# Weight buffers of one size, a separate load for each unit's last weight quarter, and modulation sums on ScalarE and POOL in a two-layer generator backbone

## The chip, the cores and the metric

The kernel runs on one core of one Trainium2 chip. The core has five engines that run side by side, each its own instructions in order: TensorE (PE; its weight loads are listed as PEld), VectorE (DVE), ScalarE (ACT), GpSimd (POOL) and SyncE (SP), which issues most DMAs. The metric is the time of one execution in device microseconds; lower is better. Three executions of the kernel before took 2499.07, 2501.16 and 2501.43 us, so the median is 2501.16 us.

## The reference

The input is a sequence of 512 latent tokens and 256 context tokens, each with 1024 channels. Two layers follow, then a final normalisation. Each layer computes:

```
sh1, sc1, g1, sh2, sc2, g2 = split(silu(c) @ w_ada[l] + b_ada[l], 6)
h = rmsnorm(x) * (1 + sc1) + sh1
y = hybrid_mixer(h, ...)
x = x + g1 * y
h = rmsnorm(x) * (1 + sc2) + sh2
x = x + g2 * ((silu(h @ w_gate) * (h @ w_up)) @ w_down)
```

The mixer has one input projection (w_in), three branches (windowed attention, a gated linear recurrence, a gated MLP over chunks), a projection of each branch (w_branch) merged by sigmoid gates, and an output projection (w_out). In layer 0 the context tokens go through the same steps with their own modulation vector from c_ctx (so there are two "batches" of modulation, b = 0 and 1); in layer 1 only the latent tokens need the FFN. All is float32. The FFN's inner width is 2816, which is 22 tiles of 128.

## The kernel before, in words

**Layout.** Activations lie channel by token: a tile has 128 channels on the partitions and up to 768 tokens along the row. A matmul takes 128 × 128 weights and up to 512 tokens.

**Three matmuls for one.** Each float32 operand is split into a high and a low part in the matmul's own format (float32r). A product is three matmuls: high weights by high activations, high by low, low by high. For weights the raw tile arrives by DMA in `wr`; ScalarE copies it into `wh`, which rounds it (L288); VectorE subtracts to get `wl` (L289). `dense` (L292) does this for one output tile of 128 channels and `kt` input tiles. For 768 tokens each input tile costs three times (512 + 256) columns of TensorE.

**Weight buffers.** `wr`, `wh` and `wl` are rings (L112 to L114) of 12, 8 and 8 KB a partition. A tile of `kt` = 8 takes 4 KB of a ring, one of 4 takes 2 KB, one of 2 takes 1 KB. A tile that comes round to memory of earlier tiles waits until their last readers are done.

**Layer 0's FFN.** The 22 inner tiles are worked in pieces of 4, 2, 4, 4, 4 and 4 (`FF_PIECES`). A piece first makes its tiles of silu(gate) × up, split in high and low (`gu`), then its down projection: eight output columns of 128 channels, `kt` = the piece's size, each followed by residual adds on VectorE (`add_res`, L780), one for the latent tokens and one for the context. The first piece is plain: gate and up tiles by `dense`. The 18 other tiles are worked in pairs by a scheme with seven products in place of eight: `seven` (L412) takes two weight tiles and two halves of the tokens as a 2 × 2 block product. One call of `seven` is called a unit here; a pair has a gate unit and an up unit.

**A unit.** It loads two raw tiles r1 and r2 of 4 KB a partition (L422); each has a weight tile's two quarters (the upper and the lower half of the input channels). POOL makes four sums, s1 to s4, in this order (L426 to L428), s1 from r2 alone, the others from r1, r2 and earlier sums. `high_low` (L341) splits four stationary tiles: g1 from r1, g2 from s2 and s1, g3 from s3 and s4, and g4 from the second half of r2, which is the last quarter (L450). `product` (L400) runs twelve matmuls of 384 columns for each of the seven products, into three PSUM accumulators, with copies by ScalarE (`ptmp`, L435 to L443) and combinations by VectorE between them. The activations' sums and differences for it come from the generator `seven_acts` (L349), which the plain piece's loop steps; its last step splits four T4 quarters over the memory of the first activation halves, and is taken at the start of the second piece (L1353).

**Modulation.** The products silu(c) @ w_ada are not matmuls, except for the first four units of layer 0. A modulation unit has 512 output columns and four steps (`ada_units`, L527); a step loads 256 rows of w_ada (512 KB, `wra`, also from the ring `wr`) and adds each half, scaled by a channel's silu(c), to an accumulator `acc` (L522 on ScalarE for the very first, L524 on VectorE for the others), for `nb` batches. After the fourth step VectorE folds `acc` down (`ada_fold`, a transpose L499 and a reduction L500 for each batch), and after the last unit `ada_spread` finishes on TensorE and VectorE. The steps wait in `ada_queue`, and `fill(n)` takes n of them wherever the program has room. During layer 0's FFN, 32 steps for layer 1 are queued (L1304): 16 with two batches (units 0 to 3), 16 with one (units 4 to 7). A step is taken after every pair of tiles (L492) and after every second column of a down projection (L1369).

**Order.** The program is written in one order; a planner at build time keeps each engine's queue, moving an instruction ahead where by its own estimate its operands come earlier, with the program's order deciding between those that are ready. On the chip the queues are in order. SP's DMA issues are such a queue too.

## Time and profile before

| | |
|---|---|
| runs, median | 2501.16 us (2499.07 to 2501.43) |
| profiled execution, whole | 2495.73 us |
| its span | 2493.9 us |
| mean granted TensorE clock | 0.992 |
| instructions | 34222 |

The profile shows one execution. Its page gives busy times by engine, 40 slices of the span, DMA queues, the chain that ended last and the costliest groups of instructions; the trace behind it answers questions for a stretch of time: a timeline, a list of waits, busy time by window, groups by shape. Matmuls are pipelined, so the durations of single matmuls overlap, and the distance of their starts is the true pace. `L306` is the matmul of `dense`, `L407` that of a unit. In a row such as `pd<-hh,wl` the output stands left of the arrow and the operands right of it. Numbers in square brackets in a timeline are the engine's idle time before the row and what ended it. Slices of 62 us of the page, TensorE, VectorE and DMA:

```profile
PE   8899999999999989989999999999999999999998
DVE  4688777875534376666656586678884547433335
DMA  8222111123523232233233252111213645233334
```

Layer 0's FFN runs from about 920 to 1480 us of the span: slices 15 to 24.

### The profile page before, as it was taken

The numbers are of one execution on the slowest core, as the hardware profiler recorded it, in microseconds if no ns is written. First come the engines' busy times: TensorE is split into PE (matmuls) and PEld (weight loads), VectorE is DVE, ScalarE is ACT, GpSimd is POOL, SyncE is SP. The second block draws the span as 40 slices with busy tenths as digits, with TensorE's granted clock in tenths as the row PEclk, the third lists the DMA queues.
The fourth block names the chain that finished last, engine by engine and source line by source line (L and its number), as shares of the span: only waits on it lengthen the run. The fifth ranks groups of instructions, "written<-read, shape, count | busy, mean of one in ns | idle before, by whom it ended". The sixth has DMA issues, their size and how long they took to land. (4 is left out here: it accounts for less than half of the span.)

```text
span 2493.9 us, 34222 instructions
## 1 busy us (share of the span) xinstructions
PE 2400.1 (96%) x13606; PEld 2084.2 (84%) x13606; DVE 1548.0 (62%) x2636; ACT 896.0 (36%) x1508; POOL 321.4 (13%) x223
## 2 busy tenths in 40 slices
PE   8899999999999989989999999999999999999998
PEld 3888888888888878879998978888888789887888
DVE  4688777875534376666656586678884547433335
ACT  3333354442222343232423453335453325322224
POOL 0000100000111230221212231000000122000001
PEclk9999999999999999999999999999999999999999
DMA  8222111123523232233233252111213645233334
GB/s 289 70 77 77 52 43 40 38 64 106 156 86 88 80 98 85 81 94 113 78 109 110 77 160 60 43 43 52 60 52 118 182 136 155 85 100 94 93 99 129
DMA packets 360080, 235.28 MB, mean 94 GB/s; under 512 B 8369, under 2 KB 331377, under 8 KB 359921
## 3 DMA queue, kind: packets, MB, share of 16 engines
q1 hardware_dynamic: 355984, 220.52, 30.0%
q0 software_dynamic: 2304, 10.49, 1.2%
q8 instruction: 107, 1.75, 0.3%
q10 hardware_dynamic: 1632, 2.10, 0.2%
q14 instruction: 53, 0.43, 0.1%
HBM read 225.73 MB, written 7.34 MB: 93 GB/s over the span
## 5 line engine op out<-in xcount | busy, mean ns | idle before, releaser
L288 ACT ACTIVATE wh<-wr 128x1024 fp32r<-128x1024 f32 (+4 forms) x344 | 306.5, 895 | 804.8 <-PE pd L306 655.9
L289 DVE TENSOR_TENSOR wl<-wr,wh 128x1024 fp32r<-128x1024 f32 (+4 forms) x344 | 353.1, 1030 | 260.4 <-ACT wh L288 257.5
L306 PE MATMUL pd<-hh,wh 128*128 128x512 f32 (+1 forms) x1504 | 458.6, 361 | 0.2 <-DVE q L793 0.2
L306 PE MATMUL pd<-hh,wl 128*128 128x512 f32 (+1 forms) x1504 | 448.3, 354 | 10.5 <-DVE wl L289 10.3
L306 PE MATMUL pd<-hl,wh 128*128 128x512 f32 (+1 forms) x1504 | 447.0, 354 | 0.0
L306 PEld LDWEIGHTS pd<-hh,wl 128*128 128x128 f32 x1504 | 248.3, 190 | 51.7 <-DVE wl L289 13.9
L306 PEld LDWEIGHTS pd<-hl,wh 128*128 128x128 f32 x1504 | 247.9, 190 | 33.8
L306 PEld LDWEIGHTS pd<-hh,wh 128*128 128x128 f32 x1504 | 248.4, 190 | 30.3 <-issue 0.9
L524 DVE SCALAR_TENSOR_TENSOR acc<-wra,sc,acc 128x512 f32<-128x512 f32 x224 | 165.9, 766 | 97.8 <-DMA wra<-in_w_ada 78.6
L306 PE MATMUL pd<-fl,wh 128*128 128x512 f32 (+1 forms) x496 | 176.8, 373 | 4.5 <-DVE fl L703 4.5
L306 PE MATMUL pd<-fh,wh 128*128 128x512 f32 (+1 forms) x496 | 175.7, 372 | 4.0 <-ACT wh L288 3.4
L306 PE MATMUL pd<-guh,wh 128*128 128x512 f32 (+1 forms) x576 | 174.4, 344 | 3.9 <-DVE X L780 1.9
L306 PE MATMUL pd<-fh,wl 128*128 128x512 f32 (+1 forms) x496 | 175.5, 371 | 0.3 <-DVE wl L289 0.3
L306 PE MATMUL pd<-guh,wl 128*128 128x512 f32 (+1 forms) x576 | 173.4, 343 | 2.4 <-DVE wl L289 2.3
L306 PE MATMUL pd<-gul,wh 128*128 128x512 f32 (+1 forms) x576 | 173.6, 342 | 0.0
L780 DVE SCALAR_TENSOR_TENSOR X<-pd,mod,X 128x256 f32<-128x256 f32 (+1 forms) x160 | 84.2, 559 | 98.9 <-PE pd L306 98.4
L306 PEld LDWEIGHTS pd<-guh,wh 128*128 128x128 f32 x576 | 99.3, 190 | 18.0 <-ACT guh L732 2.2
L306 PEld LDWEIGHTS pd<-guh,wl 128*128 128x128 f32 x576 | 99.4, 191 | 15.8 <-DVE wl L289 3.2
L306 PEld LDWEIGHTS pd<-gul,wh 128*128 128x128 f32 x576 | 99.4, 190 | 14.2 <-DVE gul L733 1.4
L306 PEld LDWEIGHTS pd<-fh,wh 128*128 128x128 f32 x496 | 89.9, 189 | 22.8 <-ACT wh L288 6.0
L306 PEld LDWEIGHTS pd<-fl,wh 128*128 128x128 f32 x496 | 90.4, 189 | 21.4 <-DVE fl L703 5.8
L652 POOL TENSOR_TENSOR sqa<-sqa,sq 128x256 f32<-128x256 f32 (+1 forms) x40 | 51.6, 1290 | 417.9 <-ACT sq L650 412.9
(285 smaller groups left out, 4478.0 us busy)
## 6 DMA issues: line engine op xcount, KB each, us to landing
wr<-in_w_in SPq DMA_DIRECT2D x116, 512.0 KB, 3.8
wra<-in_w_ada SPq DMA_DIRECT2D x80, 512.0 KB, 3.8
wr<-in_w_ffn_gate SPq DMA_DIRECT2D x44, 512.0 KB, 3.8
wr<-in_w_ffn_up SPq DMA_DIRECT2D x44, 512.0 KB, 3.9
wr<-in_w_out SPq DMA_DIRECT2D x32, 512.0 KB, 3.7
wr<-in_w_branch SPq DMA_DIRECT2D x48, 256.0 KB, 3.4
wr<-in_w_ffn_down SPq DMA_DIRECT2D x48, 256.0 KB, 3.4
wr<-in_w_ffn_down SPq DMA_DIRECT2D x24, 384.0 KB, 3.2
```

Of the source, the lines that this page charges most:

```text
L288: nc.scalar.activation(out=h, in_=r, func=AF.Copy)
L289: nc.vector.tensor_tensor(out=o, in0=r, in1=h.bitcast(F32), op=ALU.subtract)
L306: nc.tensor.matmul(ps[:, b0:b1], lhsT=w[:, k, :], rhs=x[:, b0:b1], start=b not in first, stop=(k == kt - 1 and i == 2), skip_group_check=True)
L524: nc.vector.scalar_tensor_tensor(out=acc[:, 0:512], in0=w, scalar=sc, in1=acc[:, 0:512], op0=ALU.mult, op1=ALU.add)
L652: eng.tensor_tensor(out=acc[:, c0:c1], in0=acc[:, c0:c1], in1=sq[:, c0:c1], op=ALU.add)
L780: self.nc.vector.scalar_tensor_tensor(out=self.X[m][:, c0:c1], in0=ps[:, c0:c1], scalar=gcol(b, m), in1=self.X[m][:, c0:c1], op0=ALU.mult, ...
```

## The change

- The rings become pools of fixed places: three for `wr`, two for `wh`, two for `wl`, each 4 KB a partition, with one tag, so that a smaller tile occupies a whole place (`load_raw`, `stationary`).
- A unit loads its last weight quarter a second time, as a tile r3 of its own (256 KB), and g4 is split from r3 in place of the second half of r2.
- No modulation step is taken in `seven_gate_up` any more. In layer 0 one is taken after every second column only in pieces of more than two tiles.
- The four one-batch units 4 to 7 go to a queue of their own, `pool_queue`, taken after the other columns of those pieces. Their products are made by ScalarE (into a page `acm`) and added by POOL; the first one goes straight into the accumulator. The fold of such a unit comes one step later, at the start of the next unit, with an extra step at the end. The sums of each group have a `parts` tile of their own size.
- The last step of `seven_acts` is taken at the end of the first piece's gate and up tiles, ahead of its down projection.

```diff
-        self.wr = ctx.enter_context(tc.tile_pool(name="wraw", bufs=1)).ring(3 * D * 4, name="wrawr")
-        self.wh = ctx.enter_context(tc.tile_pool(name="whi", bufs=1)).ring(2 * D * 4, name="whir")
-        self.wl = ctx.enter_context(tc.tile_pool(name="wlo", bufs=1)).ring(2 * D * 4, name="wlor")
+        self.wr = ctx.enter_context(tc.tile_pool(name="wraw", bufs=3))
+        self.wh = ctx.enter_context(tc.tile_pool(name="whi", bufs=2))
+        self.wl = ctx.enter_context(tc.tile_pool(name="wlo", bufs=2))
...
     def load_raw(self, wap, kt):
-        raw = self.wr.tile([P, kt, P], F32, name=self.nm("wr"))
+        raw = self.wr.tile([P, KD, P], F32, tag="wr", name=self.nm("wr"))[:, 0:kt, :]
...
+    def stationary(self, kt):
+        return [pool.tile([P, KD, P], F32R, tag=tag, name=self.nm(tag))[:, 0:kt, :]
+                for pool, tag in ((self.wh, "wh"), (self.wl, "wl"))]
...
         r1, r2 = (self.load_raw(w, KD).rearrange("p k c -> p (k c)") for w in (w1, w2))
+        r3 = self.load_raw(w2[KD // 2 * P:, :], KD // 2).rearrange("p k c -> p (k c)")
...
-        g4 = self.high_low(r2[:, n:2 * n])
+        g4 = self.high_low(r3)
...
             self.free(s)
-            self.fill(1)
...
-            else:
+            elif eng is None:
                 nc.vector.scalar_tensor_tensor(out=acc[:, 0:512], in0=w, scalar=sc, in1=acc[:, 0:512],
                                                op0=ALU.mult, op1=ALU.add)
+            else:
+                t = self.single("acm")
+                nc.scalar.activation(out=t[:, 0:512], in_=w, func=AF.Copy, scale=sc)
+                eng.tensor_tensor(out=acc[:, 0:512], in0=acc[:, 0:512], in1=t[:, 0:512], op=ALU.add)
+                self.free(t)
...
+            j = i if lag == 0 else i - 1
+            if q == (3 if lag == 0 else 0) and j >= 0:
+                for b, acc in enumerate(state[j]):
+                    r0 = 16 * (j * nb + b)
+                    self.ada_fold(acc, state["parts"][:, r0:r0 + 16])
...
-            self.ada_queue += self.ada_units(1, (0, 1, 2, 3), 2) + self.ada_units(1, (4, 5, 6, 7), 1)
+            self.ada_queue += self.ada_units(1, (0, 1, 2, 3), 2)
+            self.pool_queue = self.ada_units(1, (4, 5, 6, 7), 1, nc.gpsimd)
...
-            if l == 0 and f0 + n > plain:
-                if f0 <= plain:
-                    quarters, qheld = next(making)
+            if l == 0 and f0 + n == plain:
+                quarters, qheld = next(making)
+            elif l == 0:
                 self.seven_gate_up(l, range(max(f0, plain), f0 + n, 2), quarters, gu, guheld)
...
-                    if l == 1 or m % 2:
+                    if l == 1 or m % 2 and n > 2:
                         self.fill(1)
+                    elif n > 2 and self.pool_queue:
+                        self.pool_queue.pop(0)()
```

More of the change, by code (lines that the diff above doesn't have):

```diff
@@ L284, in load_w @@
         raw = self.load_raw(wap, kt)
-        hi = self.wh.tile([P, kt, P], F32R, name=self.nm("wh"))
-        lo = self.wl.tile([P, kt, P], F32R, name=self.nm("wl"))
+        hi, lo = self.stationary(kt)
         r, h, o = (t.rearrange("p k c -> p (k c)") for t in (raw, hi, lo))
@@ L529, in ada_units @@
+    def ada_units(self, l, units, nb, eng=None):
         state = {}
+        tag = "parts" if eng is None else "partsp"
+        lag = 0 if eng is None else 1
         def step(i, q):
-            u = units[i]
+            u = units[i] if i < len(units) else None
             if (i, q) == (0, 0):
-                self.parts = self.sp.tile([P, 128], F32, tag="parts", name=self.nm("parts"))
-            if q == 0:
-                state["accs"] = [self.single("acc") for _ in range(nb)]
-            raw = self.wr.tile([P, 2, 512], F32, name=self.nm("wra"))
@@ L538, in step @@
-            self.nc.sync.dma_start(out=raw, in_=self.a["w_ada"][l][q * 256:(q + 1) * 256, u * 512:(u + 1) * 512]
-                                   .rearrange("(k p) c -> p k c", p=P))
-            for k in (0, 1):
-                self.ada_accum(state["accs"], raw[:, k, :], 2 * q + k)
-            if q == 3:
-                for b, acc in enumerate(state["accs"]):
-                    r0 = 16 * (i * nb + b)
-                    self.ada_fold(acc, self.parts[:, r0:r0 + 16])
-                self.free(*state["accs"])
-                if i == len(units) - 1:
-                    self.ada_spread(l, units, self.parts, nb)
@@ L549, in ada_units @@
-        return [lambda i=i, q=q: step(i, q) for i in range(len(units)) for q in range(4)]
+                state["parts"] = self.sp.tile([P, 16 * nb * len(units)], F32, tag=tag, name=self.nm(tag))
+            if u is not None:
+                if q == 0:
+                    state[i] = [self.single("acc") for _ in range(nb)]
+                raw = self.wr.tile([P, 2, 512], F32, tag="wr", name=self.nm("wra"))
+                self.nc.sync.dma_start(out=raw, in_=self.a["w_ada"][l][q * 256:(q + 1) * 256, u * 512:(u + 1) * 512]
+                                       .rearrange("(k p) c -> p k c", p=P))
+                for k in (0, 1):
+                    self.ada_accum(state[i], raw[:, k, :], 2 * q + k, eng)
@@ new lines, in step @@
+            j = i if lag == 0 else i - 1
[3 more added lines that the diff above has]
+                    self.ada_fold(acc, state["parts"][:, r0:r0 + 16])
+                self.free(*state[j])
+                if j == len(units) - 1:
+                    self.ada_spread(l, units, state["parts"], nb)
+        steps = [(i, q) for i in range(len(units)) for q in range(4)] + [(len(units), 0)] * lag
@@ L551, in ada_first @@
+        return [lambda i=i, q=q: step(i, q) for i, q in steps]
     def ada_first(self):
```

6 lines of the change are left out of this document (2 added, 4 removed).

## The prediction

> **What bounds the kernel now.** I read the busy times first, then what TensorE waits for, then the stretches of the layer-0 FFN, the only place where the order of work changes. Busy times, page part 1:
>
> ```profile
> PE 2400.1 (96%) x13606; PEld 2084.2 (84%) x13606; DVE 1548.0 (62%) x2636; ACT 896.0 (36%) x1508; POOL 321.4 (13%) x223
> ```
>
> TensorE is the bound: 2400.1 of 2493.9 us. No edit takes a matmul away, so only its 94 us of idle time, and time at a lower clock, can move. The list of TensorE's waits from 920 to 1490 us (layer 0's FFN; us in total, times, longest), then the same list from 1049 to 1082 us, the FFN's short piece of two tiles:
>
> ```profile
> PE pa L407 <- ACT ptmp L435: 7.9, 5, 2.6
> PE pa L407 <- DVE wl L733: 7.1, 10, 1.6
> ...
> PE pd L306 <- DVE wl L289: 2.3, 1, 2.3
> PE pd L306 <- ACT guh L732: 1.9, 1, 1.9
> PE pd L306 <- DVE X L780: 1.3, 2, 0.8
> ```
>
> L407 is a product of a seven-product unit: 7.9 + 7.1 = 15.0 us are lost in the units, 2.3 + 1.9 + 1.3 = 5.5 us in and before the short piece's down projection. The longest wait, in the timeline (POOL, ACT, PE; start, us, idle before and releaser):
>
> ```profile
> 1113.17 1.87 POOL L428 TENSOR_TENSOR s<-wr 128x512 f32<-128x512 f32 x1 [17.20 <-DMA wr<-in_w_ffn_gate]
> 1118.28 1.06 ACT L732 ACTIVATE wh<-s 128x1024 fp32r<-128x1024 f32 x1 [4.63 <-POOL s L428]
> 1116.68 0.33 PE L407 MATMUL pb<-fh,wh 128*128 128x384 f32 x1
> ...
> 1117.55 0.34 PE L407 MATMUL pb<-fh,wl 128*128 128x384 f32 x1
> 1120.49 0.76 PE L407 MATMUL pa<-np,wh 128*128 128x384 f32 x2 [2.60 <-ACT ptmp L435]
> ```
>
> POOL waits for the second raw weight tile (r2) of the next gate unit, ScalarE for POOL's sums, TensorE for ScalarE (2.60). From 1116.68 to 1117.55 are five matmuls, 0.174 us each; a product of twelve takes 2.1. r2 is late because the tile whose place it takes is held until the up unit before it splits its last quarter. The waits cost clock too; granted clock by windows of 3.4 us (the column after POOL):
>
> ```profile
> 1055.90:1059.30 3.40, 3.40 (x13) 2.60 (x12) 3.10 (x5) 0.80 (x2) 0.00 (x0) 0.51 0.00 0
> 1076.40:1079.80 3.40, 3.40 (x11) 2.92 (x12) 2.15 (x5) 1.06 (x1) 0.00 (x0) 0.50 0.66 191
> 1120.80:1124.20 3.40, 3.40 (x12) 3.40 (x11) 2.35 (x3) 1.12 (x2) 0.60 (x1) 0.50 0.51 151
> 1219.80:1223.20 3.40, 3.40 (x12) 3.40 (x11) 3.40 (x12) 0.90 (x2) 2.41 (x2) 0.50 0.02 6
> ```
>
> Half clock for 3.4 us costs 1.7 us of work; four times 1.7 is 6.8 us. (The Trainium skill, "TensorE: Matmul & The Clock Gate", section "Why this matters for your kernels", asks only for no idle gaps over about 3 us; here gaps of 1.9 to 2.6 us were followed by half clock, so the rows decide, and the rule has no chance of its own. By it the change would win 6.8 us less and come out near 2517.)
>
> **What goes.** The third load r3 frees r2 as soon as POOL has summed it, so the next unit's r1 and r2 land a whole unit earlier; and the one modulation step after each pair of tiles, whose products stand in VectorE's queue ahead of weight splits (0.99 us of waiting for its DMA, then 0.75, before a split), leaves the units:
>
> ```profile
> 1097.37 0.75 DVE L524 SCALAR_TENSOR_TENSOR acc<-wra,sc,acc 128x512 f32<-128x512 f32 x1 [0.99 <-DMA wra<-in_w_ada]
> 1098.04 1.22 DVE L733 TENSOR_TENSOR wl<-wr,wh 128x1024 fp32r<-128x1024 f32 x1
> ```
>
> The short piece gets no steps at all. At most 15.0 + 5.5 + 6.8 = 27.3 us go. I take 25: a little over two of the 15 are waits at a unit's first product behind a down projection, which neither edit touches.
>
> **What comes.** The steps gather in the four down projections of four tiles before the last piece: four two-batch steps (VectorE) and four one-batch steps (ScalarE and POOL) in each, where it had four in all. And every raw tile, a down tile of 2 KB a partition too, now fills one of three 4 KB places, and one of two for wh and wl. Prices:
>
> ```profile
> wra<-in_w_ada SPq DMA_DIRECT2D x80, 512.0 KB, 3.8
> wr<-in_w_ffn_gate SPq DMA_DIRECT2D x44, 512.0 KB, 3.8
> ...
> wr<-in_w_ffn_down SPq DMA_DIRECT2D x48, 256.0 KB, 3.4
> L288 ACT ACTIVATE wh<-wr 128x512 fp32r<-128x512 f32 x96 | 60.0, 630 | 144.1 <-PE pd L306 110.2 <-DMA wr<-in_w_ffn_down 19.8 <-PE pg L407 10.5
> L289 DVE TENSOR_TENSOR wl<-wr,wh 128x512 fp32r<-128x512 f32 x96 | 68.1, 714 | 6.3 <-ACT wh L288 6.3
> L522 ACT ACTIVATE acc<-wra,sc 128x512 f32<-128x512 f32 x32 | 22.1, 718 | 33.6 <-DMA wra<-in_w_ada 31.4 <-DVE macc L1290 0.8 <-PE pd L306 0.7
> L524 DVE SCALAR_TENSOR_TENSOR acc<-wra,sc,acc 128x512 f32<-128x512 f32 x224 | 165.9, 766 | 97.8 <-DMA wra<-in_w_ada 78.6 <-ACT acc L522 18.7
> L499 DVE STREAM_TRANSPOSE tr<-acc 128x512 f32<-128x512 f32 x32 | 21.2, 691 | 0.1
> L500 DVE TENSOR_REDUCE parts<-tr 128x16 f32<-128x512 f32 x32 | 20.6, 666 | 0.2
> L780 DVE SCALAR_TENSOR_TENSOR X<-pd,mod,X 128x256 f32<-128x256 f32 x112 | 51.6, 478 | 57.0 <-PE pd L306 56.8
> L780 DVE SCALAR_TENSOR_TENSOR X<-pd,mod,X 128x512 f32<-128x512 f32 x48 | 35.9, 748 | 41.9 <-PE pd L306 41.6
> L428 POOL TENSOR_TENSOR s<-wr,wr 128x512 f32<-128x512 f32 x18 | 27.5, 1529 | 4.1 <-DMA wr<-in_w_ffn_up 4.1
> ```
>
> And one such down projection now, VectorE's first and last residual add (X) and some rows between; then the engines' busy time in it:
>
> ```profile
> 994.60 1.14 DVE L780 SCALAR_TENSOR_TENSOR X<-pd,mod,X 128x512 f32<-128x512 f32 x2 [1.06 <-PE pd L306]
> 995.66 0.68 DVE L289 TENSOR_TENSOR wl<-wr,wh 128x512 fp32r<-128x512 f32 x1
> 996.85 2.74 DVE L524 SCALAR_TENSOR_TENSOR acc<-wra,sc,acc 128x512 f32<-128x512 f32 x4 [0.51 <-DMA wra<-in_w_ada]
> ...
> 1016.86 2.25 DVE L733 TENSOR_TENSOR wl<-wr,wh 128x1024 fp32r<-128x1024 f32 x1
> ...
> 1024.28 1.14 DVE L780 SCALAR_TENSOR_TENSOR X<-pd,mod,X 128x512 f32<-128x512 f32 x2 [3.10 <-PE pd L306]
> ```
>
> ```profile
> 990.00:1023.50 33.50, 33.50 (x191) 29.00 (x190) 23.68 (x36) 5.55 (x8) 6.08 (x4) 1.00 0.33 97
> ```
>
> Seven columns in 1024.28 − 994.60: 4.24 us each, without a stall. The next unit's r1 is already being split at 1016.86, some seven microseconds ahead of need; that lead is what the small tiles buy.
>
> *Places.* A down tile holds its place 3.4 + 0.63 + 0.71 = 4.7 us, a ScalarE step's tile 3.8 + 2 × 0.72 = 5.2, a VectorE step's 3.8 + 4 × 0.77 and one column's residual adds between (0.75 + 0.48) = 8.1. Two columns need 2 × 4.7 + 5.2 + 8.1 = 22.7 us of places; three places give 3 × 8.48 = 25.4. Booked: 89%. Now it is two 2 KB tiles and one 4 KB tile in 12 KB: (2 × 2 × 4.7 + 4 × 8.1) / 12 = 4.3 of 8.48 us, 51%. VectorE's own load there is 8 × (0.75 + 0.48 + 0.71) + 14 × 0.77 + 3 folds × 1.36 = 30.4 of 33.9 us, 90%. Nothing breaks in the mean; queues form.
>
> *Start of the next unit (four times).* r2 takes the place of the last down tile. That tile's wh and wl wait for column 5 to end (two places; columns count from 0), then 0.63, residual adds 1.23, 0.71: 2.6 us. r2 lands 3.8 later; two POOL sums 3.1, wh 1.06, wl 1.22: 11.8 us after column 5. TensorE wants that wl after two columns, two products and two matmuls, 8.5 + 4.2 + 0.35 = 13.0: 1.2 us to spare, or 1.9 late with one block of four modulation products (3.06) ahead of the tile's split. VectorE is also late by itself. The last step's tile takes the place of down tile 6: column 4's end + 2.6 + 3.8, which is 2.2 us after column 5. In the 10.8 us that are left VectorE has, in program order, the block 3.06, adds 2.46, the last down split 0.71, folds 3 × 1.36 and the unit's first two splits 2.44: 12.8 us, so 2.0 late, and about 3 with a DMA wait like the 0.5 and 1.0 in the rows above. I take 3.5, between this and both latenesses together (4.9), and 1.7 of clock, since shorter gaps brought it: 4 × 5.2 = 20.8 us. Ends: 0 (as now, where the lead covers it) and 4 × (4.9 + 1.7) = 26.
>
> *Inside the down projection.* With two places for wl, a split may start when the column two before ends and is needed 4.2 + 0.7 us later; 0.63 goes to ScalarE. VectorE has 4.2 us for a block 3.06, adds 1.23, split 0.71: 5.0, over by 0.8, and by 1.9 with a DMA wait. Half of the four blocks meet it: 2 × 1.3 = 2.6 a projection, 10.4 us in all. Ends 0 and 16 × 1.9 = 30. The merge stage (595 to 850 us), with two places for wl and one such block for a gate and a branch column today, has
>
> ```profile
> PE pd L306 <- DVE wl L289: 4.9, 3, 2.5
> ```
>
> which is 1.6 us each where it happens, between my 0.8 and 1.9.
>
> *The rest.* 28 products go from VectorE (0.77 each) to ScalarE (0.72) and POOL (about 1.5, from L428): both are idle for four fifths of the row above (5.55 and 6.08 of 33.5); without cover 0.7 us each. POOL's adds slow a neighbour: the split at 1016.86 took 2.25 us beside POOL's sums, against 1.22 above. I count 3 us in all, ends −2 and 11. (The Trainium skill, "SBUF — State Buffer", section "Who interferes with whom", says that a VectorE operation with two SBUF inputs and a POOL operation that reads SBUF block each other; the 2.25 agrees.) The 18 loads r3 add 4.7 MB on SP's queue behind loads that wait for places; the units need three loads per 14.5 us, so nothing. The quarters' splits (T4), moved ahead of the first down projection, wait for the last plain unit's matmuls, as they do now: nothing. Layer 1's down projections lose a raw place but have no steps: nothing, at most 4.
>
> *Sum.* −25 + 20.8 + 10.4 + 3 = +9.2 us: on the profiled execution's 2495.7 (span 2493.9 and 1.8 around it) 2504.9; that execution was 5.4 below the median of the runs, so 2501.2 + 9.2, or 2510.
>
> **Rivals.** *Main (0.40):* as summed; its own range is 2506 to 2522.
> *The places are enough (0.25; the other side):* if modulation tiles are consumed as they land, so that r2 is issued before column 5 has ended, the start of the units costs 1 us each, the down projections 0.5 each, the rest 1: 7 − 25 = −18, 2483. It decides where the fold falls: at 12.8 us of queue in 10.8 it fails, with the folds (4.1) done earlier it holds. For it: the unstalled row of today.
> *Even (0.20):* 3 and half a clock window a start (15.4), 1 a projection (4), the rest 3, so 22.4 − 25: 2499.
> *POOL blocks VectorE (0.10):* seven adds a projection, each adding 1.0 us (2.25 − 1.22), bring VectorE to 30.4 + 7 = 37.4 of 33.9 us: 3.5 more for each, 14 in all: 2524. For it, the 2.25; against, the modulation products' mean of 766 ns.
> *r3 doesn't bring r2 forward (0.05):* POOL's sums need pages that come free no earlier; about 15 of the gain stays away: 2525.
>
> **Numbers.** Slower: 0.40 + 0.10 + 0.05 = 0.55; same: 0.20; faster: 0.25, with the line at 0.2% (5 us), about what a measurement of this kernel can tell from no change. The range runs from inside the faster case to the two slow ones: 2485 to 2527.
>
> **What would show it.** The waits for `ptmp` and `wl` in units that follow units gone; new waits of 2 to 5 us for `wh` or `wl` where a unit follows a down projection, with half clock behind; TensorE waiting for `wl` (L289's line) in those projections; SP waiting longer for modulation products. If these starts are clean, the sum of places is wrong; if the second pairs still wait, r3 is.

## The result, and the profile after

The changed kernel took 2484.41 us (median of four runs, 2477.91 to 2485.28), the kernel before in the same runs 2500.39 (2499.07 to 2501.43). The ratio is 0.9931, with a 95% interval from 0.9913 to 0.9949: **faster by 16 us, 0.7%**, where I had forecast 9 us slower. The profiled execution took 2485.11 us, its span is 2483.3. Busy times, the page's part 1:

```profile
PE 2401.9 (97%) x13606; PEld 2085.3 (84%) x13606; DVE 1533.7 (62%) x2608; ACT 919.2 (37%) x1536; POOL 368.8 (15%) x251
```

The engines do the work that the diff says: 28 modulation products left VectorE. The list of TensorE's waits from 920 to 1480 us, layer 0's FFN (us in total, times, longest):

```profile
PE pg L409 <- ACT wh L744: 7.9, 3, 3.6
PE pd L309 <- DVE wl L292: 5.1, 4, 3.3
...
PE ada L511 <- DVE parts L502: 2.8, 1, 2.8
PE pa L409 <- ACT ptmp L438: 1.2, 1, 1.2
...
PE pa L409 <- DVE wl L745: 0.8, 2, 0.5
```

L409 is the product of a unit (L407 before), L309 the matmul of `dense` (L306). The 7.9 and 7.1 us of waits inside the units are 1.2 and 0.8. New are the first and the third row: the starts of the four units that follow a down projection (in the fourth, matmuls that finish the modulation, `ada`, stand ahead of the unit and wait for the last fold). The second row has nothing to do with them: 4.6 of its 5.1 us are a wait of 1.31 us in the last column of the stage and one of 3.33 at layer 1's first projection, where the kernel before waits 4.38 us for squares of the next norm (sqa) instead. One of the four starts, in the timeline of all engines (start, us, engine; in brackets the idle time before the row and what ended it):

```profile
1155.33 6.77 SPq L279 DMA_DIRECT2D wr<-in_w_ffn_gate  x3
...
1158.97 2.74 DVE L526 SCALAR_TENSOR_TENSOR acc<-wra,sc,acc 128x512 f32<-128x512 f32 x4 [2.36 <-DMA wra<-in_w_ada]
1161.03 1.06 ACT L744 ACTIVATE wh<-wr 128x1024 fp32r<-128x1024 f32 x1 [5.33 <-DMA wr<-in_w_ffn_gate]
...
1162.47 1.29 POOL L431 TENSOR_TENSOR s<-wr 128x512 f32<-128x512 f32 x1 [6.47 <-DMA wr<-in_w_ffn_gate]
1162.67 1.29 DVE L501 STREAM_TRANSPOSE tr<-acc 128x512 f32<-128x512 f32 x2
...
1163.89 1.24 DVE L502 TENSOR_REDUCE parts<-tr 128x16 f32<-128x512 f32 x2
1165.05 1.21 DVE L745 TENSOR_TENSOR wl<-wr,wh 128x1024 fp32r<-128x1024 f32 x1
...
1165.14 1.06 ACT L744 ACTIVATE wh<-s 128x1024 fp32r<-128x1024 f32 x1 [3.06 <-DVE parts L502]
...
1166.25 1.01 PE L409 MATMUL pg<-np,wh 128*128 128x384 f32 x2 [2.24 <-ACT wh L744]
```

Two chains end together. VectorE has the block of four products, the residual adds and two folds ahead of the split of r1: its wl ends at 1165.05 + 1.21 = 1166.26. r2 landed at 1162.47, POOL's two sums took until 1165.1, and the wh made of them ends at 1165.14 + 1.06 = 1166.20. TensorE waits 2.24 us. The granted clock behind three of these starts, by windows (PE, PEld, DVE, ACT, POOL busy, then the clock):

```profile
1166.30:1169.70 3.40, 3.40 (x11) 3.40 (x12) 2.18 (x3) 0.00 (x0) 3.32 (x2) 0.50 0.28 77
1265.30:1268.70 3.40, 3.40 (x13) 3.40 (x12) 1.42 (x2) 0.47 (x1) 2.55 (x2) 0.50 0.49 143
1360.80:1364.20 3.40, 2.96 (x12) 2.96 (x13) 3.40 (x9) 1.06 (x1) 3.17 (x3) 0.51 0.01 2
1364.20:1367.60 3.40, 3.40 (x13) 3.40 (x12) 2.68 (x17) 0.00 (x0) 0.48 (x1) 0.50 0.83 235
```

The last two rows are one start: its half clock lasts 6.8 us, two windows of 3.4.

So the gain in the units came and so did the late starts. To see what else moved, I cut every profiled execution at the same matmuls (each trace lists 13606): the 3601st, 5201st, 8801st, 10801st, 12001st and the 13601st. The stretches are layer 0's merge, layer 0's FFN with the first tiles of layer 1, then layer 1's merge and FFN; in brackets stands the time at half clock, counted in windows of 3.4 us (it comes in pieces of 3.4 or 6.8 us but for the run's very end). The last columns give the median and the ratio to the kernel before, run beside it. Medians are of the fast runs; four slow ones (2533 and 6038 us of wr_ring, 4746 of raw_places_alone, 9584 of dve_units) are left out, with which those three medians would be 2494.86, 2488.86 and 2487.32.

| kernel | merge 0 | FFN 0 | merge 1 | FFN 1 | median us | ratio (95%) |
|---|---|---|---|---|---|---|
| before | 293.3 (1) | 669.8 (6) | 231.9 (1) | 334.3 | 2500.39 | |
| after | 288.5 (0) | 666.6 (8) | 237.1 (1) | 328.6 | 2484.41 | 0.9931 (0.9913 to 0.9949) |
| pools_alone | 288.4 (0) | 663.5 (4) | 238.5 (2) | 328.6 | 2485.72 | 0.9948 (0.9933 to 0.9962) |
| rings_kept | 294.0 (1) | 645.6 (2) | 239.4 (3) | 334.3 | 2482.43 | 0.9932 (0.9918 to 0.9947) |
| no_r3 | 288.4 (0) | 659.7 (7) | 238.0 (2) | 328.6 | 2480.31 | 0.9925 (0.9909 to 0.9941) |
| mod_old | 288.4 (0) | 669.4 (4) | 236.9 (1) | 328.6 | 2485.26 | 0.9944 (0.9929 to 0.9959) |
| mods_alone | 291.4 (0) | 657.5 (4) | 238.5 (2) | 334.3 | 2490.20 | 0.9961 (0.9950 to 0.9973) |
| r3_alone | 296.3 (2) | 668.4 (6) | 232.8 (0) | 334.3 | 2500.17 | 1.0003 (0.9994 to 1.0012) |
| raw_places_alone | 285.1 (0) | 669.5 (7) | 237.1 (1) | 334.4 | 2487.20 | 0.9953 (0.9937 to 0.9969) |
| wr_ring | 292.5 (1) | 663.7 (4) | 241.9 (4) | 328.6 | 2492.99 | 0.9977 (0.9966 to 0.9988) |
| wr_ring_dve | 295.5 (3) | 653.5 (4) | 239.1 (2) | 328.6 | 2485.37 | 0.9952 (0.9940 to 0.9965) |
| wh_wl_rings | 285.1 (0) | 650.8 (4) | 234.0 (0) | 334.3 | 2470.78 | 0.9895 (0.9877 to 0.9912) |
| wh_wl_no_r3 | 285.1 (0) | 649.6 (2) | 236.4 (2) | 334.3 | 2477.36 | 0.9910 (0.9892 to 0.9928) |
| wh_wl_dve | 288.4 (0) | 645.0 (3) | 235.4 (0) | 334.3 | 2468.93 | 0.9881 (0.9868 to 0.9894) |
| whole_l1 | 289.9 (1) | 653.5 (4) | 234.3 (0) | 328.6 | 2469.50 | 0.9881 (0.9864 to 0.9898) |
| lag_all | 288.5 (0) | 658.6 (3) | 240.6 (1) | 328.6 | 2480.34 | 0.9914 (0.9896 to 0.9932) |
| wl_ring | 288.4 (0) | 663.6 (8) | 237.6 (1) | 333.1 | 2487.83 | 0.9942 (0.9921 to 0.9963) |
| dve_units | 285.1 (0) | 666.8 (9) | 239.6 (2) | 328.6 | 2485.16 | 0.9938 (0.9916 to 0.9960) |
| both_gains | 289.9 (1) | 646.5 (4) | 236.0 (1) | 328.6 | 2463.16 | 0.9847 (0.9823 to 0.9872) |

From before to after, in the two profiled executions: merge 0 −4.8 us, FFN 0 −3.2, merge 1 +5.2, FFN 1 −5.7. In the merges and in layer 1's FFN nothing of the change is at work but the buffers, and my sum had no term there.

Each stretch can be taken apart further: TensorE's waits, the work lost at half clock (1.7 us a window), and the rest, which is the pace of the matmuls. FFN 0 is 35.6 + 10.2 + 624.0 us before and 29.6 + 13.7 + 623.3 after. Layer 0's merge is 6.7 + 1.7 + 284.8 before and 1.8 + 0 + 286.6 after, so waits and clock gave 6.6 us there and the pace took 1.8 back. The pace is not the change's: in dve_units, whose instructions of that stretch are the same, in the same order on TensorE, it is 283.2 (a hundred of the first thousand matmuls take 17.33 us there and 17.67 in the changed kernel). What sets it stays open; it moves a single profile by 3.4 us.

### The profile page after: what moved, and what is told of

Same layout as the page of the kernel before. It is cut to its first block, busy times and chain, and to the rows that moved or that the text cites. A ratio compares the mean times of both kernels' runs of the same rounds, so it can differ in the third digit from the quotient of the medians.

```text
span 2483.3 us, 34425 instructions
## 1 busy us (share of the span) xinstructions
PE 2401.9 (97%) x13606; PEld 2085.3 (84%) x13606; DVE 1533.7 (62%) x2608; ACT 919.2 (37%) x1536; POOL 368.8 (15%) x251
## 4 chain that ended last, share of the span: by engine, by line
PE 58%; DVE 10%; DMA 5%; issue 4%; ACT 2%; POOL 1%; POOLq 0%; DVEq 0%; ACTq 0%
PE pd L309 43%; PE pa L409 6%; DMA wra<-in_w_ada 5%; PE pg L409 3%; DVE wl L292 3%; DVE acc L526 2%; PE pb L409 1%; PE hl L857 1%; ACT wh L291 1%; DVE X L792 1%; PE pT L1117 1%; PE sc L1062 1%; DVE fl L715 1%; DVE nt L705 0%; PE pv L1108 0%
## 5 line engine op out<-in xcount | busy, mean ns | idle before, releaser
L309 PE MATMUL pd<-hh,wl 128*128 128x512 f32 (+1 forms) x1504 | 451.9, 356 | 11.0 <-DVE wl L292 11.0
L309 PE MATMUL pd<-hh,wh 128*128 128x512 f32 (+1 forms) x1504 | 459.0, 361 | 0.8 <-ACT wh L291 0.6
L309 PE MATMUL pd<-hl,wh 128*128 128x512 f32 (+1 forms) x1504 | 446.2, 353 | 0.0
L309 PEld LDWEIGHTS pd<-hh,wl 128*128 128x128 f32 x1504 | 248.4, 189 | 53.0 <-DVE wl L292 16.2
L309 PEld LDWEIGHTS pd<-hh,wh 128*128 128x128 f32 x1504 | 249.2, 190 | 33.1 <-ACT wh L291 2.0
L309 PEld LDWEIGHTS pd<-hl,wh 128*128 128x128 f32 x1504 | 247.2, 189 | 34.6
L526 DVE SCALAR_TENSOR_TENSOR acc<-wra,sc,acc 128x512 f32<-128x512 f32 x196 | 142.1, 761 | 158.7 <-DMA wra<-in_w_ada 122.8
L309 PE MATMUL pd<-fl,wh 128*128 128x512 f32 (+1 forms) x496 | 177.2, 373 | 4.6 <-DVE fl L715 4.6
L309 PE MATMUL pd<-fh,wl 128*128 128x512 f32 (+1 forms) x496 | 176.3, 372 | 0.4 <-DVE wl L292 0.3
L309 PE MATMUL pd<-fh,wh 128*128 128x512 f32 (+1 forms) x496 | 175.3, 371 | 0.6 <-ACT silu L1351 0.6
L309 PE MATMUL pd<-guh,wh 128*128 128x512 f32 (+1 forms) x576 | 174.2, 343 | 0.9 <-ACT wh L291 0.5
L309 PE MATMUL pd<-guh,wl 128*128 128x512 f32 (+1 forms) x576 | 172.8, 341 | 1.8 <-DVE wl L292 1.8
L309 PE MATMUL pd<-gul,wh 128*128 128x512 f32 (+1 forms) x576 | 173.2, 341 | 0.3 <-DVE gul L745 0.2
L309 PEld LDWEIGHTS pd<-guh,wl 128*128 128x128 f32 x576 | 98.3, 189 | 15.5 <-DVE wl L292 2.6
L309 PEld LDWEIGHTS pd<-gul,wh 128*128 128x128 f32 x576 | 98.9, 189 | 14.7 <-DVE gul L745 1.6
L309 PEld LDWEIGHTS pd<-guh,wh 128*128 128x128 f32 x576 | 98.5, 189 | 14.4 <-ACT wh L291 1.2
L309 PEld LDWEIGHTS pd<-fl,wh 128*128 128x128 f32 x496 | 90.6, 189 | 21.8 <-DVE fl L715 5.8
L309 PEld LDWEIGHTS pd<-fh,wl 128*128 128x128 f32 x496 | 90.9, 190 | 17.3 <-DVE wl L292 1.2
```

Source lines behind the costliest of these rows:

```text
L309: nc.tensor.matmul(ps[:, b0:b1], lhsT=w[:, k, :], rhs=x[:, b0:b1], start=b not in first, stop=(k == kt - 1 and i == 2), skip_group_check=True)
L526: nc.vector.scalar_tensor_tensor(out=acc[:, 0:512], in0=w, scalar=sc, in1=acc[:, 0:512], op0=ALU.mult, op1=ALU.add)
```

## The experiments

**The parts of the change, each put back or done alone.** First, the kernel before with fixed places for all three buffers (pools_alone), then the changed kernel with rings again (rings_kept), without the third load (no_r3), and with the old modulation steps (mod_old).

```diff
 pools_alone, on the kernel before (rings_kept: the reverse, on the changed one)
-        self.wr = ctx.enter_context(tc.tile_pool(name="wraw", bufs=1)).ring(3 * D * 4, name="wrawr")
+        self.wr = ctx.enter_context(tc.tile_pool(name="wraw", bufs=3))
...
 no_r3, on the changed kernel
-        r3 = self.load_raw(w2[KD // 2 * P:, :], KD // 2).rearrange("p k c -> p (k c)")
-        g4 = self.high_low(r3)
+        g4 = self.high_low(r2[:, n:2 * n])
...
 mod_old, on the changed kernel
+            self.fill(1)
-            self.ada_queue += self.ada_units(1, (0, 1, 2, 3), 2)
-            self.pool_queue = self.ada_units(1, (4, 5, 6, 7), 1, nc.gpsimd)
+            self.ada_queue += self.ada_units(1, (0, 1, 2, 3), 2) + self.ada_units(1, (4, 5, 6, 7), 1)
-                    if l == 1 or m % 2 and n > 2:
+                    if l == 1 or m % 2:
```

> The kernel before with one edit: the three rings become pools of fixed 4 KB places (three, two, two). Theory 'places help outside layer 0's FFN': the waits for wl in layer 0's merge (1.8 + 0.5 + 2.5 us and a half-clock window, together 5.7) and the 3.4 us at the returns from layer 1's down projections to its gate and up tiles go, 5 us come in layer 1's merge, and layer 0's FFN, whose units still wait for r2 and for steps, loses up to 10 from raw places held longer: 2495 to 2505. Rival 'places only cost' (the gains in the merge and in layer 1 come from elsewhere): 2505 to 2515, with the waits in layer 0's merge still there.

> The changed kernel with the rings put back; r3 and the placing of the modulation steps stay. Theory 'places help outside layer 0's FFN, and cost at the starts of its units': the starts behind the four down projections (2.1 to 3.6 us each, 15.8 with the clock) shrink to about half, the merge of layer 0 and layer 1's transitions lose 11 and layer 1's merge wins 5 again: 2480 to 2486. Rival 'places only cost': 2465 to 2475. Rival 'without places r3 helps less, since a tile comes round to memory in the order of the ring': 2490 or more, with waits for wl or ptmp inside the units.

> The changed kernel without the third load: g4 is split from the second half of r2 again. Theory 'r2 held until g4 makes the next unit's r2 late': the units that follow another unit wait for ptmp and wl again, about 10 of the 15 us and some half clock come back: 2494 to 2500. Rival 'the modulation steps in the units made them wait': 2483 to 2487, no waits inside the units.

> The changed kernel with the modulation steps where they were: one after each pair of tiles, one after every second column of every down projection, all products on VectorE; pools, r3 and the earlier T4 splits stay. Theory 'the steps gathered in the down projections make the next unit's start late': the four starts lose their 2.1 to 3.6 us waits and the half clock (up to 15.8 us less), while a step between the units costs what it did, 3 to 8 us: 2474 to 2482. Rival 'the units need VectorE and the places free of steps': 2490 to 2500, with waits for ptmp and wl in the units.

Measured: 2485.72, 2482.43, 2480.31 and 2485.26 us. Each of the four is within 5 us of the whole change, so its parts do not add. Places alone give most of it (13.4 us below the kernel before that ran beside them), with 6.3 us from layer 0's FFN, which no theory of mine had. Rings kept give as much, but from one stretch: FFN 0 falls by 24.2 us. Its waits there, TensorE's list from 920 to 1480 us, hold no start of a unit at all (gul is the low part of silu(gate) × up, X the residual):

```profile
PE pd L309 <- DVE gul L745: 2.9, 4, 0.9
PE pd L309 <- DVE X L792: 1.1, 2, 0.8
```

Against rings, fixed places cost layer 0's FFN 666.6 − 645.6 = 21.0 us, and what they give lies in the other stretches. Without the third load the waits in the units did not come back, against my theory; the starts were late by 7.7 us in sum, not 10.7. With the old steps neither theory's time came: the late starts went, and the units waited 7.6 us for wl in their place.

**The third load and the moved steps, each with rings.** mods_alone is rings_kept without r3; r3_alone is the kernel before with r3 as its one edit.

> The kernel before with the modulation steps placed and made as in the change (none in the units, one-batch ones on ScalarE and POOL) and the earlier T4 splits; rings, and no third load. Theory 'the steps in the units, not the hold on r2, made the units wait' (places without the third load had no such waits either): the 15.0 us of waits for ptmp and wl and the 5.5 of the short piece go, 2478 to 2486. Rival 'r2 held until the last quarter is split makes the next unit late': about 10 of the 15 us and their half clock stay, 2488 to 2494.

> The kernel before with one edit: the third load. Theory 'the steps in the units made them wait': the waits inside the units stay at 10 to 15 us, 2495 to 2502. Rival 'r2 held until the last quarter is split makes the next unit late': they fall below 5 us, 2484 to 2491.

2490.20 and 2500.17 us: the third load alone does nothing. Its list for layer 0's FFN shows the waits of the units as they were (L407 is a unit's product):

```profile
PE pa L407 <- ACT ptmp L436: 8.5, 5, 2.6
PE pa L407 <- DVE wl L734: 6.0, 8, 1.1
```

and that of mods_alone shows them nearly gone, with others in the down projections:

```profile
PE pd L309 <- DVE X L791: 4.8, 5, 1.6
...
PE pd L309 <- DVE gul L744: 4.4, 5, 1.3
PE pa L409 <- DVE wl L744: 2.0, 4, 1.0
PE pa L409 <- ACT ptmp L437: 1.4, 2, 1.0
```

So with the steps between the units they wait, 14.5 us even with r3, and without the steps 3.4. The earlier T4 splits, which mods_alone has too, are not the reason: mod_old keeps them, and with the steps back its units waited for wl again. But the hold on r2 is not disproved. The split of the last quarter and the issue of the next gate unit's r2, first in the kernel before, then in r3_alone (there two loads, r3 at 1110.78 and r2 at 1111.46):

```profile
1107.94 0.69 DVE L733 TENSOR_TENSOR wl<-wr,wh 128x512 fp32r<-128x512 f32 x1 [2.29 <-ACT wh L732]
1108.66 0.37 SPq L279 DMA_DIRECT2D wr<-in_w_ffn_gate  x1
```

```profile
1110.74 0.69 DVE L734 TENSOR_TENSOR wl<-wr,wh 128x512 fp32r<-128x512 f32 x1
1110.78 1.05 SPq L279 DMA_DIRECT2D wr<-in_w_ffn_gate  x2
```

In both, r2 is issued 0.03 us after that split ends. In r3_alone the split reads r3, which lies in the same ring: r2's load now waits for the split of r3 and is as late as before (the wait behind it is 2.60 us in both). A step's tile, also in the ring, is loaded between the two units in both kernels. Without it (mods_alone) most of the wait is gone though r2 is held as before, so the hold cost what it did together with the step.

The time of mods_alone lies in the rival's range all the same, because 9.2 us of waits for X and gul came. With the steps gone, r3 on top gives 657.5 − 645.6 = 11.9 us in FFN 0, 3.4 of it half clock; the waits for X and gul fall to 4.0. How the third load shortens those was not taken apart.

**Which buffer.** wr_ring is the changed kernel with a ring for raw tiles alone, wh_wl_rings with rings for wh and wl alone, raw_places_alone the kernel before with fixed places for raw tiles alone, wl_ring the changed one with a ring for wl alone.

```diff
 wr_ring
-        self.wr = ctx.enter_context(tc.tile_pool(name="wraw", bufs=3))
+        self.wr = ctx.enter_context(tc.tile_pool(name="wraw", bufs=1)).ring(3 * D * 4, name="wrawr")
...
 wh_wl_rings
-        self.wh = ctx.enter_context(tc.tile_pool(name="whi", bufs=2))
-        self.wl = ctx.enter_context(tc.tile_pool(name="wlo", bufs=2))
+        self.wh = ctx.enter_context(tc.tile_pool(name="whi", bufs=1)).ring(2 * D * 4, name="whir")
+        self.wl = ctx.enter_context(tc.tile_pool(name="wlo", bufs=1)).ring(2 * D * 4, name="wlor")
```

> The changed kernel with the raw tiles' buffer (wr) a ring again; wh and wl keep two fixed places. With rings for all three, layer 0's FFN lay 24 us below the kernel before and no unit started late behind a down projection; with places for all it lay only 3 to 4 below; but the places took 4 to 6 us of waits for wl out of layer 0's merge and 5.7 us of waits for wh out of layer 1's FFN. Theory 'raw places cost the lead of the next unit's loads, places for wh and wl pay elsewhere': starts clean, merge and layer 1 as with places: 2470 to 2476, below every kernel so far. Rival 'two places for wh and wl make the starts late': 2481 to 2486, with waits of 2 to 3.5 us at the starts behind the four down projections.

> The changed kernel with rings for wh and wl and fixed places for raw tiles, the mirror of the run before. Theory 'raw places cost the lead': starts behind the four down projections still 2 to 3.5 us late, and the waits for wl in layer 0's merge and for wh (3.4 us in six) in layer 1's FFN are back: 2486 to 2494. Rival 'two places for wh and wl make the starts late': starts clean, 2479 to 2484.

> The kernel before with one edit: fixed places for the raw tiles only; wh and wl stay rings, the modulation steps and the second half of r2 as before. Theory 'in a ring of raw tiles the loads of the modulation steps land later than VectorE's queue has them, and splits stand behind them' (with raw places the two waits of about 1.8 us for wl in layer 0's merge were gone, with a ring they were there in each kernel): the merge of layer 0 is 5 to 8 us shorter, the units' waits in its FFN stay: 2489 to 2495. Rival 'raw places help only where the steps have been moved': 2496 to 2502.

> The changed kernel with a ring for wl alone; raw tiles and wh keep fixed places. Theory 'either of the two holds the last down tile until column 5 has ended': wh's places are enough for it, the starts stay 2 to 3.5 us late: 2482 to 2486. Rival 'only the split into wl counts, since it is the raw tile's last reader': starts clean, 2466 to 2473.

2492.99, 2470.78, 2487.20 and 2487.83 us. My theory for the first pair fell: with the steps moved, places for the raw tiles are the good part, those for wh and wl the bad one in layer 0's FFN (in layer 1's they are worth 5.7 us, below). Behind the four down projections no first product of a unit waits more than 0.4 us in either kernel of the pair, so a late start needs places for raw tiles and for wh and wl together. In wr_ring the product that needs r2's sums still waits, 4.7 us in the four units (for ptmp and wl). This fits the chain of the prediction, where r2 takes the place of the last down tile, which waits for wh and wl, which wait for column 5; either edit opens it. One link is looser than I had it. In the start shown above column 5 ended at about 1154.5, but the last tile's split into wh waited last for the tile's own load, whose place a block of products had held until 1152.27:

```profile
1155.06 0.63 ACT L291 ACTIVATE wh<-wr 128x512 fp32r<-128x512 f32 x1 [1.59 <-DMA wr<-in_w_ffn_down]
```

In layer 0's FFN wh_wl_rings is 666.6 − 650.8 = 15.8 us below the changed kernel: 6.8 of waits, 6.8 of half clock and 2.1 of pace. The late starts' 10.7 us of waits are gone, but its down projections wait 6.7 us for gul and X, which the changed kernel's don't. With a ring for wl alone the wh places hold the last tile as before, and the starts are late again; its list, layer 0's FFN:

```profile
PE pg L409 <- ACT wh L744: 6.1, 3, 3.1
```

What the raw places give is seen in layer 0's merge. Before, VectorE and ScalarE (wh) and then TensorE's wait:

```profile
756.00 1.06 ACT L288 ACTIVATE wh<-wr 128x1024 fp32r<-128x1024 f32 x1 [0.55 <-PE pd L306]
...
760.37 2.08 DVE L524 SCALAR_TENSOR_TENSOR acc<-wra,sc,acc 128x512 f32<-128x512 f32 x3 [3.92 <-DMA wra<-in_w_ada]
762.36 1.22 DVE L289 TENSOR_TENSOR wl<-wr,wh 128x1024 fp32r<-128x1024 f32 x1
...
763.64 0.62 PE L306 MATMUL pd<-hh,wl 128*128 128x512 f32 x2 [2.52 <-DVE wl L289]
```

wh was done at 757.06, but in VectorE's queue a modulation block that waits 3.92 us for its load stands ahead of the split. The same place in raw_places_alone, VectorE:

```profile
749.94 1.23 DVE L289 TENSOR_TENSOR wl<-wr,wh 128x1024 fp32r<-128x1024 f32 x1 [0.52 <-ACT wh L288]
...
754.26 0.68 DVE L289 TENSOR_TENSOR wl<-wr,wh 128x512 fp32r<-128x512 f32 x1
758.74 0.75 DVE L524 SCALAR_TENSOR_TENSOR acc<-wra,sc,acc 128x512 f32<-128x512 f32 x1 [3.79 <-DMA wra<-in_w_ada]
```

VectorE waits as long for the load, but both splits are done: with another buffer the planner wrote another order. The 4.9 us of waits for wl in this stretch are gone in every kernel with raw places; rings_kept still has 4.3 of them, wr_ring 3.6.

**Why the raw ring is slow with places for wh and wl.** In wr_ring no unit starts late behind the four down projections, and yet its FFN 0 takes 663.7 us. Its timeline in a down projection:

```profile
1154.88 3.05 POOL L531 TENSOR_TENSOR acc<-acc,acm 128x512 f32<-128x512 f32 x2 [2.93 <-ACT acm L530]
1154.99 4.14 DVE L526 SCALAR_TENSOR_TENSOR acc<-wra,sc,acc 128x512 f32<-128x512 f32 x3
...
1159.06 1.13 DVE L792 SCALAR_TENSOR_TENSOR X<-pd,mod,X 128x512 f32<-128x512 f32 x2
...
1160.33 0.47 PE L309 MATMUL pd<-guh,wh 128*128 128x512 f32 x1 [1.18 <-DVE X L792]
```

Three products take 4.14 us beside two of POOL's adds. Without such a neighbour three take 2.08, in the merge rows of the kernel before above (760.37). The edit of wr_ring_dve, wh_wl_dve and dve_units puts the one-batch products back on VectorE, at the same places:

```diff
-            elif eng is None:
+            elif eng is None or eng is nc.vector:
...
-            self.pool_queue = self.ada_units(1, (4, 5, 6, 7), 1, nc.gpsimd)
+            self.pool_queue = self.ada_units(1, (4, 5, 6, 7), 1, nc.vector)
```

> The changed kernel with a ring for the raw tiles alone (the run that took 2494.9 us, 12.4 above the one with three rings), here with the one-batch products on VectorE. In that run a product on VectorE took 1019 ns in the mean between 920 and 1480 us, against 768 in the changed kernel, and one block of three took 4.14 us while POOL made two adds. Theory 'POOL's adds, where they fall beside VectorE's products, slow these and so the residual adds and the down projection': the mean falls to about 750 ns, TensorE's waits for X (5.7 us) go, 2480 to 2487. Rival 'the raw ring's late loads cost it': 2491 to 2497, waits for X stay.

> The changed kernel, its places kept, with the one-batch products on VectorE at the same places in the program. Theory 'ScalarE and POOL take work that VectorE has no room for': 28 products of 0.77 us back, starts later by up to 5 us each: 2490 to 2505. Rival 'POOL's adds cost as much as they save': 2480 to 2486; with raw places and rings for wh and wl the same edit moved the time by less than 2 us.

> The kernel with raw places and rings for wh and wl, its one-batch modulation products back on VectorE at the same places in the program (28 products, 0.77 us each, 5.4 us more for each of four down projections). Theory 'VectorE has no room there (I had put it at 30.4 of 33.9 us)': waits of TensorE for X or wl in the down projections, 2476 to 2486. Rival 'the block of products is as short as its merged row says (2.74 us for four) and VectorE keeps up': 2468 to 2473.

2485.37, 2485.16 and 2468.93 us. For wr_ring the theory held: 7.6 us less (10.2 in FFN 0 of the two profiles), and no wait for X. The mean of a product from 920 to 1480 us (groups by line and shape; busy, mean ns), first wr_ring, then wr_ring_dve, then the changed kernel:

```profile
L526 DVE SCALAR_TENSOR_TENSOR acc<-wra,sc,acc 128x512 f32<-128x512 f32 x56 | 54.9, 1019 | 18.5 <-DMA wra<-in_w_ada 18.2 <-ACT acc L524 0.3
```

```profile
L526 DVE SCALAR_TENSOR_TENSOR acc<-wra,sc,acc 128x512 f32<-128x512 f32 x84 | 60.4, 747 | 15.3 <-DMA wra<-in_w_ada 14.6 <-ACT acc L524 0.2
```

```profile
L526 DVE SCALAR_TENSOR_TENSOR acc<-wra,sc,acc 128x512 f32<-128x512 f32 x56 | 39.8, 768 | 17.6 <-DMA wra<-in_w_ada 17.3 <-ACT acc L524 0.3
```

VectorE does 28 products more in wr_ring_dve for 5.5 us more busy time. In the changed kernel the adds happen to fall beside other work, and dve_units is not to be told from it: its starts are 12.2 us late in sum against 10.7, its interval overlaps. With rings for wh and wl the medians (2470.78 and 2468.93) have overlapping intervals too, but the profiles repeat what wr_ring shows: FFN 0 falls from 650.8 to 645.0 us, and its waits for gul and X from 6.7 to 1.3. In wh_wl_rings one product took 1.78 us (at 1126.43) beside an add of POOL (1125.81 to 1127.66), and the split into gul behind it ended a wait of 1.02. The same edit on whole_l1 (both_gains, below) takes FFN 0 from 653.5 to 646.5. So making the one-batch products on ScalarE and POOL cost FFN 0 6 to 10 us in three pairs of profiles, and gave nothing in the fourth, the changed kernel.

**The starts: folds or r2.** lag_all keeps the places and folds units 0 to 3 one step later.

```diff
-        lag = 0 if eng is None else 1
+        lag = 0 if l == 0 or units[0] > 3 and eng is None else 1
```

> The changed kernel, its places kept, with the folds of the two-batch units (0 to 3) one step later too: they leave the last column of a down projection for the second column of the next. Theory 'VectorE's queue of adds, folds and splits ahead of the unit makes its start late' (my prediction's: 12.8 us of queue in 10.8, 4.1 of it folds): the waits of 2.1 to 3.6 us at the starts fall below 1, 2470 to 2477. Rival 'r2 sets the start': its place comes free after the last down tile's split, and three loads are then under way at once (r2 landed 6.1 us after its issue, not 3.8): the starts stay, 2482 to 2487.

2480.34 us, between the two theories. No single wait at a start is over 1.2 us any more, but a wait of 2.70 us for wl came inside one down projection (it moves the work behind it, too), and waits of about 1 us inside units. Its list, layer 0's FFN:

```profile
PE pa L409 <- ACT ptmp L438: 3.6, 4, 1.2
PE pa L409 <- DVE wl L745: 3.4, 7, 1.1
...
PE pd L309 <- DVE wl L292: 2.9, 2, 2.7
```

FFN 0 is 8.0 us shorter than in the changed kernel: 3.9 less of waits and 8.5 less of half clock (three windows for eight), while the pace takes 4.4 back. So VectorE's queue, folds included, was one of the two chains, and its removal alone does not bring what the rings bring. The medians' intervals overlap. 3.7 us of the waits that are left in the four units lie at the product that needs r2's sums, but POOL began two of these sums when a VectorE instruction released it, not when r2 landed: what r2's landing is worth by itself stays open.

**The third load, and whole tiles in layer 1.** wh_wl_no_r3 is wh_wl_rings without r3; whole_l1 lets each wh and wl tile of layer 1's FFN take 4 KB of its ring; both_gains is whole_l1 with the products on VectorE.

```diff
 whole_l1, on wh_wl_rings
     def stationary(self, kt):
-        return [pool.tile([P, kt, P], F32R, name=self.nm(tag))
+        size = KD if self.whole else kt
+        return [pool.tile([P, size, P], F32R, name=self.nm(tag))[:, 0:kt, :]
                 for pool, tag in ((self.wh, "wh"), (self.wl, "wl"))]
...
         act2, hheld = self.norm_end()
+        self.whole = l == 1
```

> The kernel with raw places and rings for wh and wl, here without the third load (g4 from the second half of r2). The third load was worth 8 us with three rings and moved steps (2490.2 to 2482.4), nothing in the kernel before (2500.2) and minus 4 with places for all (2480.3 to 2484.4). Theory 'it frees r2 a unit earlier wherever the starts are not late': 2475 to 2480. Rival 'with raw places it takes a place itself and gives nothing': 2466 to 2472.

> The kernel with raw places and rings for wh and wl, where in layer 1's FFN alone each wh and wl tile takes a whole 4 KB of its ring. Theory 'the six waits for wh in layer 1's FFN (0.9 and 0.2 us at each of three returns from a down projection) come of 4 KB tiles that lie over the ends of two small ones': they go, as with places, and 3.4 to 5.7 us with them: 2464 to 2468. Rival 'they come of something else': 2470 to 2472, waits still there.

> Raw places, rings for wh and wl, whole 4 KB tiles of these in layer 1's FFN, and the one-batch products on VectorE. Theory 'the two gains lie at different places (layer 1's FFN, layer 0's down projections) and add': 2462 to 2467. Rival 'the edit on VectorE gives nothing by itself': 2466 to 2471.

2477.36, 2469.50 and 2463.16 us. Without r3 the six runs go from 2468.8 to 2482.4 and FFN 0 is 649.6 against 650.8 us: inconclusive, and no gain of r3 in the trace. In layer 1's FFN the kernel before has, at the three returns from a down projection to gate and up tiles (TensorE's waits from 2100 to 2480 us):

```profile
PE pd L306 <- ACT wh L288: 3.4, 6, 0.9
```

With whole tiles they are gone and the stretch takes 328.6 us, as with places, not 334.3: so it is the mixing of 4 KB and smaller tiles in the wh and wl rings that cost 5.7 us there (3.4 of waits, the rest pace). The medians do not settle what it is worth in all: that of whole_l1 is 1.3 us under that of wh_wl_rings (in its profile merge 0 and FFN 0 are 4.8 and 2.7 us longer), and the interval of both_gains just overlaps with that of wh_wl_dve (ratios 0.9847 and 0.9881). Both_gains has the lowest median, **2463.16 us, 1.5% below the kernel before** (ratio 0.9847, 0.9823 to 0.9872), below both kernels of this study. The longest wait that is left in its FFN 0 is one of 4.4 us for the squares of the next norm, as in the kernel before; those for the low parts of the activations at its start (fl) sum to 4.6, and every kernel has some.

## Why the prediction was wrong, step by step

**What goes, −25: right in size, half wrong in cause.** With rings kept, r3 and the moved steps take 24.2 us from FFN 0: 16.2 of waits, 6.8 of half clock, 1.1 of pace. But r3 alone left 14.5 of the 15.0 us of waits in the units, and moving the steps alone left 3.4. The step "r3 frees r2, so the next unit's r1 and r2 land a whole unit earlier" failed: with the ring, r2's load then waited for the split of r3 itself. That no_r3 has no such waits either shows that the third load was not needed for this gain.

**Start of the next unit, +20.8: right, a fifth too much.** The four waits are 2.13, 2.24, 3.56 and 2.80 us, 10.7 in sum, with half clock behind three, one of them two windows long: 10.7 + 4 × 1.7 = 17.5. I had three folds of 1.36 in VectorE's queue; the rows show two of each, 1.29 + 1.24. And I had r2 landing 3.8 us after its issue; with the last step's load, r1 and r2 issued within 1.8 us (1154.87, 1155.33, 1156.63), r1 and r2 each took 5.7 us (to 1161.03 and 1162.32).

**Inside the down projection, +10.4: the term that failed most.** It measured 0: in none of the four does TensorE wait at all. VectorE there, and ScalarE's split in front of VectorE's, in the changed kernel:

```profile
1149.53 2.74 DVE L526 SCALAR_TENSOR_TENSOR acc<-wra,sc,acc 128x512 f32<-128x512 f32 x4 [1.27 <-DMA wra<-in_w_ada]
1150.27 0.63 ACT L291 ACTIVATE wh<-wr 128x512 fp32r<-128x512 f32 x1 [3.35 <-PE pd L309]
1152.19 1.13 DVE L792 SCALAR_TENSOR_TENSOR X<-pd,mod,X 128x512 f32<-128x512 f32 x2
1153.25 1.59 DVE L292 TENSOR_TENSOR wl<-wr,wh 128x512 fp32r<-128x512 f32 x1
```

Four products in a row take 2.74 us and two adds 1.13, since neighbours overlap; I had added up single means to 3.06 and 1.23, though merged rows of 2.74 and 1.14 stood in my own fences. With these, 2.74 + 1.13 and a split of 0.68 make 4.55 us. And the time was 4.9 us from a column's end to the need, not the 4.2 that I left after taking ScalarE's 0.63 off: the rows show that split (1150.27) beside VectorE's block, which had begun 0.7 us before column 4 ended. So even a split of 1.59 us, slowed beside an add of POOL, ended at 1154.84, ahead of the matmul that reads it (1155.37). The term was made of an excess of 0.8 us that only the added means and the subtracted 0.63 had.

**Places elsewhere: missing, −10.5 us.** My sum had the buffers cost in layer 0's FFN and nothing anywhere else ("nothing, at most 4" for layer 1's down projections). Layer 0's merge became 4.8 us shorter and layer 1's FFN 5.7 us (layer 1's merge became 5.2 longer, see below). Both were in the profile of before as waits, 4.9 us for wl, which I quoted, as a price for blocks and not as a loss that could go, and 3.4 us for wh, which I did not look for. This step and the one before it turned the sign.

**The rest, +3.** It measured 666.6 − 669.8 = −3.2 for the whole stretch, less −24.2 and +17.5: 3.5 us. Against rings_kept, where the −24.2 stand, these are 2.0 of waits in the short piece's unit (0.5) and the first unit behind it (1.2 and 0.3), 1.5 more of waits in the last down projection and the step into layer 1 (6.2 for 4.7), 3.4 of half clock at 923.9 us, less 4.2 of waits for gul, X and wl that rings_kept has in the down projections and a unit; 0.8 is left open. The ScalarE and POOL sums (dve_units) gave nothing that can be told from zero, as I had counted them. The T4 step was not tried by itself.

**The sum with what was measured.** −24.2 + 17.5 + 0 + 3.5 − 4.8 − 5.7 = −13.7. Layer 1's merge gives back 5.2 in the two profiled executions and the first 3600 matmuls win 2.0, which makes the −10.6 between the two spans; the medians are 16.0 apart. Layer 1's merge stays open: of its 5.2 us, 2.0 are waits and 3.2 pace, and the 231.9 us of the profile of before are the shortest of all nineteen. Its waits there met one window of half clock, behind the longest (2.17 us); one of 1.52 met none (second row):

```profile
1933.00:1936.40 3.40, 3.23 (x8) 2.57 (x9) 1.76 (x4) 0.00 (x0) 1.64 (x1) 0.52 0.97 283
1984.80:1988.20 3.40, 1.89 (x8) 1.58 (x9) 3.32 (x5) 0.00 (x0) 0.60 (x1) 1.00 0.12 36
```

Kernels that leave that stage's code alone (mods_alone, rings_kept) take 6.6 and 7.5 us more there.

**The rivals.** "The places are enough" gave the time that came (2483) for another reason: its condition, starts of 1 us, did not hold. That its time came was luck. But the point at which I had it decide did hold: with the folds taken out of the queue (lag_all), no wait at a start is over 1.2 us. "POOL blocks VectorE" did not happen in the changed kernel, and was worth 7.6 us in wr_ring. "r3 doesn't bring r2 forward" was right in r3_alone, by the ring and not by POOL's pages, and without the price that I gave it.

## What to carry to other kernels

A buffer's shape changed the order that the planner wrote in stages that no edit touched, so when a buffer changes, list the waits of all its stages, not only of the stage that is being edited. Neither form of buffer was better everywhere here. Fixed places won for the raw tiles, though a down tile fills half of one. For wh and wl two fixed places tied a load to the end of a column in layer 0's FFN, where a ring lets small tiles run ahead; in layer 1's FFN whole 4 KB tiles beat mixed sizes in a ring. And when a term rests on an excess of less than a microsecond, build it from merged rows of the very sequence, not from the means of single instructions.

## What the runs showed of the hardware

A scalar_tensor_tensor of 128 × 512 on VectorE takes 0.75 us, and 1.38 us (a third of 4.14) while POOL adds tiles of the same size; over layer 0's FFN the mean was 1019 ns with such adds (wr_ring) and 747 without (wr_ring_dve), and the stretch 10.2 us longer. (The Trainium skill, "SBUF — State Buffer", section "Who interferes with whom", has the two engines block each other; this agrees, and the price depends on what falls beside what: in the changed kernel the same adds left the mean at 768.)

A wait did not always cost clock: of four starts with 2.13 to 3.56 us of waiting, the one of 2.13 met no half clock, while in the kernel before one of 1.82 (at 643.9 us, half clock from 646.3) did. Half clock came in pieces of 3.4 us or 6.8 (at a run's end also others), and each 3.4 us cost 1.7. The profiles hold 7 to 15 such windows, so differences of 3 to 5 us between two single profiles carry this.
